# Softmax over a diagonal of dot products: whole-batch loads of x, half-batch loads of y, and one VectorE instruction for each row

## The chip, the cores and the metric

The kernel runs on one core of one Trainium2 chip. The metric is the device time of one execution in microseconds (us); each kernel is run several times, and the median is compared. The core has 16 DMA engines, which bring data from the chip's main memory (HBM) into the on-chip memory (SBUF, 128 partitions), and several compute engines of which this kernel uses VectorE (DVE), ScalarE (ACT) and GpSimd (POOL). SyncE (SP) computes nothing here; its queue issues the loads.

## The reference

```python
B, N, D = 8, 4096, 512            # x and y are [B, N, D], float32
gram = np.matmul(x, y.transpose(0, 2, 1))
diag = np.diagonal(gram, axis1=1, axis2=2)
diag = diag - diag.max(axis=-1, keepdims=True)
exp = np.exp(diag)
return exp / exp.sum(axis=-1, keepdims=True)
```

Only the diagonal of the product is used, so row n of a batch needs one dot product of 512 elements, x[b, n] . y[b, n]. A softmax over the 4096 dot products of each batch follows. The inputs are 2 x 64 MB (134.22 million bytes together), the output is 8 x 4096 numbers. Every input byte is used once.

## The kernel before

A batch of 4096 rows lies over 128 partitions, R = 32 consecutive rows on each. A partition's share of one tensor and one batch is thus 32 x 512 x 4 bytes = 64 KB, and it lies in one piece in HBM. The kernel handles a batch in two halves of H = 16 rows for each partition. For each half, `load` allocates a tile of x and one of y (32 KB in a partition each, 4 MB over all) and issues their loads on SP's queue, x at line 43 and y at line 44. The pool `io` has three buffers for each of the two, so SP can be up to three halves ahead. A load into a buffer waits until the instructions that read its former content are done.

The products and sums are made on VectorE in one of two ways. `dots` multiplies the whole half in one instruction, in place into the x tile (line 50), and adds up over the 512 elements in a second one (line 51). `dots_by_row` does each row of the half in one instruction that multiplies and accumulates (line 58), 16 instructions for a half. The last three halves go by row, all others by `dots`. The column of dot products goes to the tile `diag`, which keeps all batches.

After both halves of a batch, `softmax` takes the maximum over each partition (line 72, VectorE), over the partitions (line 74, GpSimd), negates it (line 76), takes the exponential with its sum (line 78, ScalarE), sums over the partitions (line 83, GpSimd), takes the reciprocal and scales (lines 85 and 86), and stores 16 KB from ScalarE's queue (line 87). These steps stand in VectorE's order between the products of one batch and those of the next.

The last two halves are loaded in pieces, so that little is left to do when the last bytes land: 8 and 8 rows for the first half of the last batch, and 8, 4, 2, 1 and 1 rows for its second half.

The order on each engine is the order of the program. The framework sets the semaphores; those for the ends of DMAs are eight, reused in turn, and a DMA that takes one up again waits until the DMA that had it before has landed. Both SP's loads and ScalarE's stores take from these eight.

Of the kernel before, what the change touches and what calls it, by code (L numbers as in the profile page):

```python
# [1 line left out]

# [5 lines left out]


@with_exitstack
def kernel(
    ctx: ExitStack,
    tc: tile.TileContext,
    x: bass.AP,
    y: bass.AP,
    out: bass.AP,
):
    nc = tc.nc
    f32 = mybir.dt.float32  # L20
    B, N, D = x.shape
    P = nc.NUM_PARTITIONS
    R = N // P
    H = R // 2


    xv = x.rearrange("b (p r) d -> b p r d", p=P)
    yv = y.rearrange("b (p r) d -> b p r d", p=P)
    ov = out.rearrange("b (p r) -> b p r", p=P)

    io = ctx.enter_context(tc.tile_pool(name="io", bufs=3))
    persist = ctx.enter_context(tc.tile_pool(name="persist", bufs=1))
    sm = ctx.enter_context(tc.tile_pool(name="sm", bufs=2))

    diag = persist.tile([P, B * R], f32, name="diag")
    res = persist.tile([P, B * R], f32, name="res")

    def load(b, r0, parts):
        xt = io.tile([P, H, D], f32, tag="xt", name="xt")
        yt = io.tile([P, H, D], f32, tag="yt", name="yt")  # L40
        o = 0
        for n in parts:
            nc.sync.dma_start(out=xt[:, o : o + n, :], in_=xv[b, :, r0 + o : r0 + o + n, :])  # L43
            nc.sync.dma_start(out=yt[:, o : o + n, :], in_=yv[b, :, r0 + o : r0 + o + n, :])  # L44
            o += n
        return xt, yt

    def dots(b, r0, xt, yt):
        c = b * R + r0
        nc.vector.tensor_tensor(out=xt, in0=xt, in1=yt, op=mybir.AluOpType.mult)  # L50
        nc.vector.tensor_reduce(  # L51
            out=diag[:, c : c + H], in_=xt, axis=mybir.AxisListType.X, op=mybir.AluOpType.add
        )

    def dots_by_row(b, r0, xt, yt):
        for k in range(H):
            c = b * R + r0 + k
            nc.vector.scalar_tensor_tensor(  # L58
                out=xt[:, k, :],
                in0=xt[:, k, :],  # L60
                scalar=1.0,
                in1=yt[:, k, :],
                op0=mybir.AluOpType.mult,
                op1=mybir.AluOpType.mult,
                accum_out=diag[:, c : c + 1],
            )

    def softmax(b):
        db = diag[:, b * R : (b + 1) * R]
        rb = res[:, b * R : (b + 1) * R]  # L70
        mxp = sm.tile([P, 1], f32, tag="mxp", name="mxp")
        nc.vector.tensor_reduce(out=mxp, in_=db, axis=mybir.AxisListType.X, op=mybir.AluOpType.max)  # L72
        mx = sm.tile([P, 1], f32, tag="mx", name="mx")
        nc.gpsimd.partition_all_reduce(out_ap=mx, in_ap=mxp, channels=P, reduce_op=bass_isa.ReduceOp.max)  # L74
        nmx = sm.tile([P, 1], f32, tag="nmx", name="nmx")
        nc.vector.tensor_single_scalar(out=nmx, in_=mx, scalar=-1.0, op=mybir.AluOpType.mult)  # L76
        sump = sm.tile([P, 1], f32, tag="sump", name="sump")
        nc.scalar.activation(  # L78
            out=rb, in_=db, func=mybir.ActivationFunctionType.Exp,
            bias=nmx, scale=1.0, accum_out=sump,  # L80
        )
        ssum = sm.tile([P, 1], f32, tag="ssum", name="ssum")
        nc.gpsimd.partition_all_reduce(out_ap=ssum, in_ap=sump, channels=P, reduce_op=bass_isa.ReduceOp.add)  # L83
        rc = sm.tile([P, 1], f32, tag="rc", name="rc")
        nc.vector.reciprocal(out=rc, in_=ssum)  # L85
        nc.vector.tensor_single_scalar(out=rb, in_=rb, scalar=rc, op=mybir.AluOpType.mult)  # L86
        nc.scalar.dma_start(out=ov[b], in_=rb)

    for b in range(B):
        for h in range(2):  # L90
            n = 2 * b + h
            parts = {2 * B - 2: [8, 8], 2 * B - 1: [8, 4, 2, 1, 1]}.get(n, [H])
            xt, yt = load(b, h * H, parts)
            (dots_by_row if n >= 2 * B - 3 else dots)(b, h * H, xt, yt)
        softmax(b)


# [1 line left out]
_INS = ['x', 'y']  # L99
_OUTS = [((8, 4096), 'float32')]  # L100


# [23 lines left out]
```

## Time and profile before

| | |
|---|---|
| device time, median of 3 runs | 323.48 us (323.29 to 323.94) |
| the profiled execution's own time | 323.94 us |
| its span, first to last instruction | 321.6 us |
| VectorE busy | 261.4 us, 81% of the span |
| ScalarE, GpSimd busy | 4.6 us, 6.1 us |
| moved by DMA | 134.36 MB, mean 418 GB/s over the span |
| loads issued by SP | 28 of 4 MB, 6 of 2 MB, 8 smaller |
| median time from issue to landing, 4 MB | 31.2 us (x), 40.5 us (y) |
| stores | 8 of 16 KB, median 12.9 us to landing |

The profile is of one execution. Its times are in microseconds from the start of the span; "busy" is the time in which an engine executes, and a line such as "L50" is the line of the program that made the instruction. A timeline row gives the start, the duration, the engine, the line, the operation with its output and inputs, and, in brackets, how long the engine stood idle before it and what ended that. "SPq" rows are the issue of a transfer, not the transfer itself. The difference between device time and span, 2.3 us here, lies outside the first and the last instruction.

### The profile page before, as it was taken

How to read it: one execution, taken by the hardware profiler on the slowest of the kernel's cores; microseconds unless marked ns; L12 is line 12 of the kernel's file. 1: busy time of each engine (PE TensorE's matmuls, PEld its weight loads, DVE VectorE, ACT ScalarE, POOL GpSimd, SP SyncE). 2: the span in 40 equal slices, each digit the busy share in tenths (PEclk: the TensorE clock that was granted, in tenths of full speed). 3: DMA queues.
4: the chain of work that ended last, by engine and by line, in shares of the span. 5: the costliest groups of instructions: out<-in, count | busy, mean ns of one | idle time of the engine just before them, and what ended most of it. 6: DMA issues, size and time to landing. Idle time of an engine off the chain costs nothing.

```text
span 321.6 us, 345 instructions
## 1 busy us (share of the span) xinstructions
DVE 261.4 (81%) x154; ACT 4.6 (1%) x17; POOL 6.1 (2%) x20
## 2 busy tenths in 40 slices
DVE  0019979898998979979799897989979799776494
ACT  1000000000000000000000000000000000000000
POOL 0000000000000000000000000000000000000000
DMA  8999999999999999999999999999999999999991
GB/s 326 456 395 452 440 408 456 391 458 391 456 412 436 454 395 456 440 408 458 416 432 456 392 458 440 408 456 417 433 449 395 456 437 412 424 424 426 427 407 53
DMA packets 7201, 134.36 MB, mean 418 GB/s; under 512 B 1824, under 2 KB 1824, under 8 KB 2592
## 3 DMA queue, kind: packets, MB, share of 16 engines
q1 hardware_dynamic: 6048, 134.22, 97.5%
q10 hardware_dynamic: 1152, 0.13, 0.3%
q14 instruction: 1, 0.01, 0.0%
HBM read 134.22 MB, written 0.13 MB: 418 GB/s over the span
## 4 chain that ended last, share of the span: by engine, by line
DMA 63%; DVE 33%; issue 1%; SPq 1%; POOL 1%; ACT 0%; POOLq 0%; DVEq 0%
DMA yt<-in_y_dram 63%; DVE xt L50 16%; DVE diag L51 16%; SPq L43 1%; POOL mx L74 0%; POOL ssum L83 0%; DVE mxp L72 0%; DVE xt L58 0%; ACT res L78 0%; DVE rc L85 0%; POOLq L121 0%; SPq L44 0%; DVE res L86 0%; DVE nmx L76 0%; DVEq L50 0%
## 5 line engine op out<-in xcount | busy, mean ns | idle before, releaser
L50 DVE TENSOR_TENSOR xt<-xt,yt 128x8192 f32<-128x8192 f32 x13 | 113.0, 8689 | 34.5 <-DMA yt<-in_y_dram 34.5
L51 DVE TENSOR_REDUCE diag<-xt 128x16 f32<-128x8192 f32 x13 | 112.9, 8686 | 0.4
L58 DVE SCALAR_TENSOR_TENSOR xt<-xt,yt 128x512 f32<-128x512 f32 x48 | 30.0, 687 | 9.9 <-DMA yt<-in_y_dram 9.7
L74 POOL PARTITION_ALL_REDUCE mx<-mxp x8 | 2.8, 352 | 306.6 <-DVE mxp L72 306.6
L85 DVE RECIPROCAL rc<-ssum 128x1 f32<-128x1 f32 x8 | 1.3, 164 | 7.7 <-POOL ssum L83 7.7
L78 ACT ACTIVATE res<-diag,nmx 128x32 f32<-128x32 f32 x8 | 2.6, 321 | 312.9 <-DVE nmx L76 312.9
L76 DVE TENSOR_SCALAR nmx<-mx 128x1 f32<-128x1 f32 x8 | 1.2, 154 | 4.3 <-POOL mx L74 4.3
L58 DVE DVE_READ_ACCUMULATOR xt<-xt,yt 128x1 f32 x48 | 3.9, 82 | 0.0
L83 POOL PARTITION_ALL_REDUCE ssum<-sump x8 | 3.1, 385 | 5.8 <-ACT res L78 5.8
L86 DVE TENSOR_SCALAR res<-res,rc 128x32 f32<-128x32 f32 x8 | 1.9, 242 | 0.9
L72 DVE TENSOR_REDUCE mxp<-diag 128x1 f32<-128x32 f32 x8 | 1.5, 186 | 0.3
L78 ACT ACTIVATION_READ_ACCUMULATOR res<-diag,nmx 128x1 f32 x8 | 1.5, 186 | 0.0
L78 ACT ACT_TABLE_LOAD x1 | 1.3, 1283 | 0.7 <-PEq L110 0.7
L110 POOL MEMSET const-float32-0.0<- 128x1 f32 x1 | 0.1, 100 | 0.2 <-issue 0.2
L110 POOL MEMSET const-bfloat16-1.0<- 128x1 bf16 x1 | 0.1, 102 | 0.0
L110 POOL MEMSET const-uint8-127<- 128x1 uint8 x1 | 0.1, 102 | 0.0
L110 POOL MEMSET const-float32-1.0<- 128x1 f32 x1 | 0.1, 99 | 0.0
## 6 DMA issues: line engine op xcount, KB each, us to landing
xt<-in_x_dram SPq DMA_DIRECT2D x14, 4096.0 KB, 31.2
yt<-in_y_dram SPq DMA_DIRECT2D x14, 4096.0 KB, 40.5
xt<-in_x_dram SPq DMA_DIRECT2D x3, 2048.0 KB, 27.1
yt<-in_y_dram SPq DMA_DIRECT2D x3, 2048.0 KB, 31.6
xt<-in_x_dram SPq DMA_DIRECT2D x1, 1024.0 KB, 31.9
yt<-in_y_dram SPq DMA_DIRECT2D x1, 1024.0 KB, 29.5
xt<-in_x_dram SPq DMA_DIRECT2D x1, 512.0 KB, 25.8
yt<-in_y_dram SPq DMA_DIRECT2D x1, 512.0 KB, 22.2
```

The costliest lines, as they stand in the source:

```text
L43: nc.sync.dma_start(out=xt[:, o : o + n, :], in_=xv[b, :, r0 + o : r0 + o + n, :])
L50: nc.vector.tensor_tensor(out=xt, in0=xt, in1=yt, op=mybir.AluOpType.mult)
L51: nc.vector.tensor_reduce(out=diag[:, c : c + H], in_=xt, axis=mybir.AxisListType.X, op=mybir.AluOpType.add)
L58: nc.vector.scalar_tensor_tensor(out=xt[:, k, :], in0=xt[:, k, :], scalar=1.0, in1=yt[:, k, :], op0=mybir.AluOpType.mult, op1=mybir.AluOpT ...
L72: nc.vector.tensor_reduce(out=mxp, in_=db, axis=mybir.AxisListType.X, op=mybir.AluOpType.max)
L74: nc.gpsimd.partition_all_reduce(out_ap=mx, in_ap=mxp, channels=P, reduce_op=bass_isa.ReduceOp.max)
L76: nc.vector.tensor_single_scalar(out=nmx, in_=mx, scalar=-1.0, op=mybir.AluOpType.mult)
L78: nc.scalar.activation(out=rb, in_=db, func=mybir.ActivationFunctionType.Exp, bias=nmx, scale=1.0, accum_out=sump,)
L83: nc.gpsimd.partition_all_reduce(out_ap=ssum, in_ap=sump, channels=P, reduce_op=bass_isa.ReduceOp.add)
L85: nc.vector.reciprocal(out=rc, in_=ssum)
L86: nc.vector.tensor_single_scalar(out=rb, in_=rb, scalar=rc, op=mybir.AluOpType.mult)
L110: nc = _bacc.Bacc("TRN2", target_bir_lowering=False, num_devices=1)
```

## The change

The tile of x now holds a whole batch (64 KB in a partition), is loaded by one DMA of 8 MB for the first seven batches, and has two buffers. The tile of y still holds a half (32 KB in a partition) and now has two buffers instead of three. On SP the loads of a batch are x, then the two halves of y. For the last batch x is loaded in pieces too, each ahead of its piece of y: 16 rows for the first half, then 8, 4, 2, 1 and 1 rows for the second. All halves are done by row (new line 47); the product is written in place into the y tile instead of the x tile. The two-instruction form is gone. The softmax is the same; its lines move up by 11.

```diff
--- before.py
+++ after.py
@@ -28,36 +28,25 @@
     yv = y.rearrange("b (p r) d -> b p r d", p=P)
     ov = out.rearrange("b (p r) -> b p r", p=P)
 
-    io = ctx.enter_context(tc.tile_pool(name="io", bufs=3))
+    io = ctx.enter_context(tc.tile_pool(name="io", bufs=2))
     persist = ctx.enter_context(tc.tile_pool(name="persist", bufs=1))
     sm = ctx.enter_context(tc.tile_pool(name="sm", bufs=2))
 
     diag = persist.tile([P, B * R], f32, name="diag")
     res = persist.tile([P, B * R], f32, name="res")
 
-    def load(b, r0, parts):
-        xt = io.tile([P, H, D], f32, tag="xt", name="xt")
-        yt = io.tile([P, H, D], f32, tag="yt", name="yt")
-        o = 0
-        for n in parts:
-            nc.sync.dma_start(out=xt[:, o : o + n, :], in_=xv[b, :, r0 + o : r0 + o + n, :])
-            nc.sync.dma_start(out=yt[:, o : o + n, :], in_=yv[b, :, r0 + o : r0 + o + n, :])
-            o += n
-        return xt, yt
+    def load_x(b, xt, r0, n):
+        nc.sync.dma_start(out=xt[:, r0 : r0 + n, :], in_=xv[b, :, r0 : r0 + n, :])
+
+    def load_y(b, yt, r0, o, n):
+        nc.sync.dma_start(out=yt[:, o : o + n, :], in_=yv[b, :, r0 + o : r0 + o + n, :])
 
     def dots(b, r0, xt, yt):
-        c = b * R + r0
-        nc.vector.tensor_tensor(out=xt, in0=xt, in1=yt, op=mybir.AluOpType.mult)
-        nc.vector.tensor_reduce(
-            out=diag[:, c : c + H], in_=xt, axis=mybir.AxisListType.X, op=mybir.AluOpType.add
-        )
-
-    def dots_by_row(b, r0, xt, yt):
         for k in range(H):
             c = b * R + r0 + k
             nc.vector.scalar_tensor_tensor(
-                out=xt[:, k, :],
-                in0=xt[:, k, :],
+                out=yt[:, k, :],
+                in0=xt[:, r0 + k, :],
                 scalar=1.0,
                 in1=yt[:, k, :],
                 op0=mybir.AluOpType.mult,
@@ -87,11 +76,19 @@
         nc.scalar.dma_start(out=ov[b], in_=rb)
 
     for b in range(B):
+        last = b == B - 1
+        xt = io.tile([P, R, D], f32, tag="xt", name="xt")
+        if not last:
+            load_x(b, xt, 0, R)
         for h in range(2):
-            n = 2 * b + h
-            parts = {2 * B - 2: [8, 8], 2 * B - 1: [8, 4, 2, 1, 1]}.get(n, [H])
-            xt, yt = load(b, h * H, parts)
-            (dots_by_row if n >= 2 * B - 3 else dots)(b, h * H, xt, yt)
+            yt = io.tile([P, H, D], f32, tag="yt", name="yt")
+            o = 0
+            for n in [8, 4, 2, 1, 1] if last and h == 1 else [H]:
+                if last:
+                    load_x(b, xt, h * H + o, n)
+                load_y(b, yt, h * H, o, n)
+                o += n
+            dots(b, h * H, xt, yt)
         softmax(b)
```

## The prediction

> **What bounds the kernel now.** I read the page first. Section 1 for the engines, section 2 for whether the transfers ever pause, section 3 for how they are cut.
>
> ```profile
> DVE 261.4 (81%) x154; ACT 4.6 (1%) x17; POOL 6.1 (2%) x20
> ...
> DMA  8999999999999999999999999999999999999991
> ...
> q1 hardware_dynamic: 6048, 134.22, 97.5%
> ```
>
> VectorE works 81% of the span, but the row of DMA tenths is at 9 from the second slice to the one before the last: the 16 DMA engines hardly rest. The load queue q1 moves 134.22 MB in 6048 packets. The program issues 42 loads, and 6048 / 42 = 144 = 128 + 16: one packet for each partition's run, and one small one for each DMA engine. So a packet is a run, 8 runs per DMA engine and load, and its length is what the kernel chose: 32 KB for 28 of the loads.
>
> Next the timeline of VectorE and of SP's queue in a steady stretch.
>
> ```profile
> 157.83 0.42 SPq L44 DMA_DIRECT2D yt<-in_y_dram  x1
> ...
> 159.17 8.69 DVE L50 TENSOR_TENSOR xt<-xt,yt 128x8192 f32<-128x8192 f32 x1 [1.75 <-DMA yt<-in_y_dram]
> ...
> 178.89 8.68 DVE L50 TENSOR_TENSOR xt<-xt,yt 128x8192 f32<-128x8192 f32 x1
> 187.61 8.69 DVE L51 TENSOR_REDUCE diag<-xt 128x16 f32<-128x8192 f32 x1
> ...
> 198.05 8.69 DVE L50 TENSOR_TENSOR xt<-xt,yt 128x8192 f32<-128x8192 f32 x1 [1.76 <-DMA yt<-in_y_dram]
> ...
> 236.93 8.69 DVE L50 TENSOR_TENSOR xt<-xt,yt 128x8192 f32<-128x8192 f32 x1 [1.75 <-DMA yt<-in_y_dram]
> ```
>
> Once a batch VectorE stands still and starts when y lands. These starts are 38.88 us apart, twice (198.05 - 159.17, 236.93 - 198.05): the beat of the transfers, 19.44 us for 8 MB of x and y (16 runs of 32 KB per DMA engine). The load issued at 157.83 is the one that lands for 198.05: it stood some 20 us behind another 8 MB. That is why the chain of waits shows 33% DVE and yet VectorE does not set the pace: an earlier issue would only stand longer in line.
>
> Last the end, where the runs become short.
>
> ```profile
> 276.67 0.69 DVE L58 SCALAR_TENSOR_TENSOR xt<-xt,yt 128x512 f32<-128x512 f32 x1 [2.07 <-DMA yt<-in_y_dram]
> ...
> 277.29 0.69 DVE L58 SCALAR_TENSOR_TENSOR xt<-xt,yt 128x512 f32<-128x512 f32 x1
> ...
> 296.27 0.69 DVE L58 SCALAR_TENSOR_TENSOR xt<-xt,yt 128x512 f32<-128x512 f32 x1 [2.43 <-DMA yt<-in_y_dram]
> ...
> 305.98 0.69 DVE L58 SCALAR_TENSOR_TENSOR xt<-xt,yt 128x512 f32<-128x512 f32 x1 [4.72 <-DMA yt<-in_y_dram]
> ...
> 316.15 0.69 DVE L58 SCALAR_TENSOR_TENSOR xt<-xt,yt 128x512 f32<-128x512 f32 x1 [0.50 <-DMA yt<-in_y_dram]
> ```
>
> From 276.67 to 296.27, 19.60 us, the same 8 MB arrive, now in runs of 16 KB (32 per DMA engine): 0.16 us more than 19.44, for 16 more packets and two more loads. So one packet more costs about 0.01 us; its bytes cost the rest. That is the price the whole forecast rests on. VectorE waits 4.72 us before 305.98 and 0.50 us before the last row at 316.15, so the last landing sets the end; the softmax and the store behind it take 321.6 - 316.15 = 5.45 us, and are untouched.
>
> **The change part by part.** The sum is made against the profiled execution: span 321.6, device time 323.94, 2.3 us outside the span. It is the slowest of the three runs shown (median 323.48, 0.46 less). 0.2% is 0.65 us, the spread of these runs, and about what a measurement can tell.
>
> *Runs of 64 KB for x.* Seven batches load x in 8 runs of 64 KB per DMA engine instead of 16 of 32 KB: 56 packets fewer, at 0.01 us, -0.56 us. No run here has a packet over 32 KB, so this is bounded. Best: -0.56, the step from 16 to 32 KB once more. Middle: the run goes out as two packets of 32 KB, 0. Worst: it is cut small. The nearest row is the last 8 rows of the batch, in runs of 8, 4 and 2 KB: 305.98 to 316.15 is 10.17 us where 8 rows at the steady beat take 9.72, so 4.6% more; on the x half of seven batches (7 x 19.44 = 136 us) that is +6.3 us. I take -0.56: the trace shows one packet for each run at every length used, and time per byte falling with length.
>
> *The last batch.* Its first half goes from two pieces of 8 rows to one of 16: 16 packets and two loads fewer, the measured 0.16 us the other way. *Fewer loads.* 7 more x loads disappear, 7 x 0.01 = -0.07 us (0 if nothing).
>
> [...]
>
> *VectorE.* The pair L50 and L51 costs 8.7 + 8.7 = 17.4 us per half. By row, starts are 277.29 - 276.67 = 0.62 us apart and 0.61 further on, 16 rows 9.8 us. In all 256 x 0.61 + 6 for the softmax = about 162 us instead of 261. All of it lies beside the transfers: a gain of 99 us on the engine, 0 on the path. [...]
>
> *Buffers and waits.* Can the queue now run empty? On SP the order becomes x0, y0a, y0b, x1, then y1a (waits until VectorE has left y0a), y1b (y0b), x2 (x0 free at the same moment), and so on. With 9.72 us per 4 MB: y0a lands near 32, its rows end near 42, and y1a is issued then, while x1 still streams until about 61: 19 us in hand. So in every batch, since x of the next batch always stands ahead. At the end x comes in pieces: y of the last batch's first half is issued when the y tile two back is done, near 275, with only its own x half before it, 9.7 us in hand; the 8 rows of y of the second half near 285, with some 14 us in hand. Each issue takes about 0.4 us. Cost 0; if VectorE were slower than 9.7 us per half plus that reserve, the shortfall would come straight on the path.
>
> *Semaphores of SP's loads.* They are reused every eight DMAs, the stores included. New is that a one-row piece of y near the end waits for the store of the seventh batch. It is issued near 288; the median store takes 12.9 us to land, so near 301, and the last y piece waits anyway for the 8-row piece, 10 us before the end, as it does now (305.98). Cost 0. A store that meets 64 KB packets may take up to twice as long, 26 us; only earlier batches' stores do, and nobody near them waits.
>
> *The end.* 16 rows by row (9.8 us) between landings 20 and 10.2 us before the end finish in time; 8, 4, 2 and 1 rows follow as now, and the 0.50 us wait before the last row is the cover. Cost 0, and up to 0.3 us if that cover is used up twice.
>
> *Sum:* -0.56 - 0.16 - 0.07 = -0.79 us. Span 321.6 to 320.8; profiled time 323.94 to 323.15; against the median 323.48 to **322.7 us**.
>
> **The rivals.**
>
> *Nothing to tell.* The change mainly frees VectorE, which is not the bound; if the long runs go out as two packets each, only the last batch gains: -0.16 - 0.07, 323.3 us. The saturated DMA row speaks for it, and the packet count per run against it. Also on this side: one step of the trace is 0.8 us late without a row that explains it (starts at 236.93 and 257.18, 20.25 us instead of 19.44); such a slip in some runs hides a gain of this size.
>
> *Slower: 64 KB packets stream at a lower rate than 32 KB ones.* Place: the x half of seven batches, 136 us. Each 1% costs 1.36 us, against 0.23 gained elsewhere: 323.48 - 0.23 + 1.36 = 324.6 us at 1%. Break-even is at 0.17%, and it is slower by over 0.2% from about 0.65%. No row excludes it, since no run is that long; the rows against it are those at 16 and 32 KB, where longer was quicker. Cut small, at 4.6%, it would be near 329.6.
>
> *VectorE as bound again or an empty queue.* At 0.61 us a row it would need three times the time per half to use up 19 us; I give it no chance of its own.
>
> **How the numbers follow.** Forecast (one packet per long run, -0.79): 0.58. Nothing to tell: 0.20. Slower: 0.22. The forecast lies only 0.14 us beyond the line of -0.65, so with the runs' scatter about 0.09 of its chance falls within 0.2%: 0.49 is left for faster. Of the rivals, 0.03 goes to faster for a slip that vanishes (0.01 from the second case, 0.02 from slower): faster 0.52, same 0.09 + 0.19 = 0.28, slower 0.20. The range starts at 321.9, where the 0.8 us slip also vanishes, and reaches to 324.4, which takes in the second case and slower packets up to about 0.85%. The likeliest case alone: 322.2 to 323.2.
>
> **What would show it.** Right: q1 with 33 loads and 7 x (128 + 16) + 26 x (128 + 16) = 4752 packets (5648 if long runs are split in two, far more if cut small); batch to batch starts of VectorE 38.79 us apart; the last batch's first 8 MB in 19.44 us; VectorE near 162 us busy; the last row near 315.4; the DMA row at 9 throughout. Wrong: a beat over 38.88 (slower packets), DMA tenths below 9 in the middle (an empty queue), or rows at the end that do not wait for a landing.

## The result, and the profile after

The changed kernel takes 325.14 us (median of 4 runs, 325.10 to 325.49) against 323.53 us before. The ratio is 1.0051, with a 95% interval of 1.0034 to 1.0068: half a percent slower, where 0.79 us less was forecast. The profiled execution took 325.13 us, its span is 323.1 us.

The page of the changed kernel, sections 1 to 3, the lines that answer to those shown of before, and one more:

```profile
DVE 163.9 (51%) x544; ACT 4.6 (1%) x17; POOL 6.1 (2%) x20
...
DMA  9899999899999999899999999899999899999980
...
q1 hardware_dynamic: 4752, 134.22, 96.6%
...
q14 instruction: 4, 0.03, 0.0%
```

VectorE is busy 163.9 us and the load queue moves 4752 packets, both as forecast; a 64 KB run is one packet (the packet records have 896 of 64 KB, 128 for each of the seven loads of 8 MB). The DMA row has six eights, the row of before one, in its first slice. The forecast had named such slices as the sign of an empty queue; they are none here, since the fastest kernel below has three of them too. New is the last line. Queue q14, whose kind the page calls instruction, moved 4 packets of 8 KB within the span; such a packet is called a block below. The same line of before, not shown in the forecast:

```profile
q14 instruction: 1, 0.01, 0.0%
```

The timeline of VectorE, changed kernel, at the instructions that wait for y of a batch's first half, and at the last row:

```profile
71.66 0.69 DVE L47 SCALAR_TENSOR_TENSOR yt<-xt,yt 128x512 f32<-128x512 f32 x1 [17.22 <-DMA yt<-in_y_dram]
...
110.38 0.69 DVE L47 SCALAR_TENSOR_TENSOR yt<-xt,yt 128x512 f32<-128x512 f32 x1 [16.72 <-DMA yt<-in_y_dram]
...
150.25 0.69 DVE L47 SCALAR_TENSOR_TENSOR yt<-xt,yt 128x512 f32<-128x512 f32 x1 [17.78 <-DMA yt<-in_y_dram]
...
188.98 0.69 DVE L47 SCALAR_TENSOR_TENSOR yt<-xt,yt 128x512 f32<-128x512 f32 x1 [16.64 <-DMA yt<-in_y_dram]
...
228.83 0.69 DVE L47 SCALAR_TENSOR_TENSOR yt<-xt,yt 128x512 f32<-128x512 f32 x1 [16.89 <-DMA yt<-in_y_dram]
...
267.59 0.69 DVE L47 SCALAR_TENSOR_TENSOR yt<-xt,yt 128x512 f32<-128x512 f32 x1 [16.67 <-DMA yt<-in_y_dram]
...
317.68 0.69 DVE L47 SCALAR_TENSOR_TENSOR yt<-xt,yt 128x512 f32<-128x512 f32 x1 [0.58 <-DMA yt<-in_y_dram]
```

The steps between batches are 38.72 (71.66 to 110.38), 39.87, 38.73, 39.85 and 38.76 us. Three of them are within 0.1 us of the 38.79 forecast; two are 1.1 us longer. The DMA view cut to the stretch 121 to 124 us, inside the first long step (columns: packets, MB, share):

```profile
q1 hardware_dynamic: 29, 1.90, 147.6%
q14 instruction: 1, 0.01, 0.7%
```

The trace's packet records put the four q14 packets at 48.3, 122.0, 195.8 and 271.9 us. Each of the two long steps holds one; the first packet falls into the step before the rows shown (32.42 to 71.66, 39.24 us), the fourth behind 267.59. In the kernel before the single one is at 241.1 us: inside the step from 236.93 to 257.18 that was 0.8 us late without a row to explain it.

The transfers' end, in the view by stretches (columns: stretch, its length, busy time and instructions of VectorE, ScalarE, GpSimd, granted clock, DMA share, GB/s):

```profile
306.00:311.00 5.00, 5.00 (x17) 0.00 (x0) 0.00 (x0) 1.00 1.00 407
311.00:313.50 2.50, 2.50 (x9) 0.00 (x0) 0.00 (x0) 1.00 1.02 377
314.30:317.10 2.80, 2.79 (x10) 0.00 (x0) 0.00 (x0) 1.00 0.06 25
```

In the last 2.8 us the DMA share is 0.06, which is 1/16: one DMA engine works alone, 15 are done. So the transfers did not get slower as a whole. One DMA engine fell behind, and since every load spreads over all 16 (144 packets, 9 x 16), each landing waited for that one.

The packet records allow this to be followed. Each load gives each DMA engine 8 packets of one size and one of 4 bytes, in a known order, so the packets can be chained engine by engine. The middle of the 16 engines ended its loads at 314.66 us before and at 313.58 us in the changed kernel, 1.1 us earlier. The last engine ended 1.0 us behind the middle before, and 3.6 us behind it after. Until the first q14 packet it was 0.2 us ahead of the middle; then its lag rises in steps, to 0.7, 1.7, 2.7 and 3.7 us, after the first, second, third and fourth q14 packet, and stays level between them.

The records also show what a step is made of. The q14 packet itself takes 0.31 to 0.33 us of its DMA engine. The load packet right behind it on that engine takes 1.88 us instead of 1.21 (32 KB), or 3.03 and 3.08 us instead of 2.42 (64 KB). Together that is 0.9 to 1.0 us. No other load packet of the changed kernel after the first 21 us is more than 0.25 us above the median of its size. Why the packet behind is slower is not shown.

### The profile page after: what moved, and what is told of

It is laid out like the page before. It is cut to its first block, busy times and chain, and to the rows that moved or that the text cites. A ratio compares the mean times of both kernels' runs of the same rounds, so it can differ in the third digit from the quotient of the medians.

```text
span 323.1 us, 714 instructions
## 1 busy us (share of the span) xinstructions
DVE 163.9 (51%) x544; ACT 4.6 (1%) x17; POOL 6.1 (2%) x20
## 3 DMA queue, kind: packets, MB, share of 16 engines
q1 hardware_dynamic: 4752, 134.22, 96.6%
## 4 chain that ended last, share of the span: by engine, by line
DMA 73%; DVE 25%; issue 1%; POOLq 0%; SPq 0%; POOL 0%; DVEq 0%
DMA yt<-in_y_dram 73%; DVE yt L47 25%; POOLq L118 0%; SPq L39 0%; POOL mx L63 0%; DVE res L75 0%; DVE mxp L61 0%; DVE rc L74 0%; DVEq L47 0%; DVEq L75 0%; POOLq L63 0%
## 5 line engine op out<-in xcount | busy, mean ns | idle before, releaser
L47 DVE SCALAR_TENSOR_TENSOR yt<-xt,yt 128x512 f32<-128x512 f32 x256 | 157.9, 687 | 143.8 <-DMA yt<-in_y_dram 143.8
L47 DVE DVE_READ_ACCUMULATOR yt<-xt,yt 128x1 f32 x256 | 21.0, 82 | 0.0
```

Of the source, the lines that this page charges most:

```text
L47: nc.vector.scalar_tensor_tensor(out=yt[:, k, :], in0=xt[:, r0 + k, :], scalar=1.0, in1=yt[:, k, :], op0=mybir.AluOpType.mult, op1=mybir.A ...
```

## The experiments

Theory 1: the 8 KB packets of q14 bring VectorE's instructions during the run, so that more rows mean more blocks; a block costs one DMA engine the 0.9 to 1.0 us read above, and as long as the queue stays full, this engine does not catch up. Theory 2: the long runs or the new order of loads make one engine lag. Theory 3: VectorE's traffic by row disturbs the transfers. The edits are shown shortened. Each kernel was timed beside the kernel before, whose median was 323.36 to 323.53 us every time.

**The long runs with the old VectorE mix.** Changed kernel, plus

```diff
+    def dots_pair(b, r0, xt, yt):      # tensor_tensor into yt, then tensor_reduce
-            dots(b, h * H, xt, yt)
+            (dots if 2 * b + h >= 13 else dots_pair)(b, h * H, xt, yt)
```

> The loads of the changed kernel, but the first 13 halves go by two instructions (product into the y tile, then the sum), the last 3 by row, as in the kernel before: 154 VectorE rows in the profile instead of 544. Theory 1 (instruction blocks: each 8 KB block that queue q14 brings delays one DMA engine by 0.8 to 1.0 us, and the lag stays to the end): q14 back to 1 packet, batch beat 38.80 us, median 323.53 - 0.8 = 322.7 us. Theory 2 (the 64 KB runs or the new load order let one DMA engine fall behind): 325.1 us, the last 3 us with one engine alone as in the changed kernel. Theory 3 (by-row VectorE traffic disturbs the transfers): 322.7 us too, so this run does not tell 1 from 3.

Measured: 323.99 us, from 322.58 to 325.13 over 12 runs; ratio 1.0012 (1.0000 to 1.0024). q14 fell to 1 packet, but only the fastest runs came to the 322.7 expected. This fits no theory as it stood. At the end one engine is late again:

```profile
315.00:316.00 1.00, 1.00 (x5) 0.00 (x0) 0.00 (x0) 1.00 0.06 25
```

SP's timeline has the issue of y for the 15th half:

```profile
282.65 0.33 SPq L42 DMA_DIRECT2D yt<-in_y_dram  x1
```

It is issued at 282.65 us, because the 13th half (two instructions, 17.4 us) holds its y buffer until then. The x half ahead of it runs out near 284, so the queue is all but empty. Whether that is the cause is tested further down, under "The old mix with the queue kept full".

**The old loads with every half by row.** Kernel before, with

```diff
-            (dots_by_row if n >= 2 * B - 3 else dots)(b, h * H, xt, yt)
+            dots_by_row(b, h * H, xt, yt)
```

> The kernel before with every half by row; loads and buffers untouched: 544 VectorE rows. Theory 1: q14 4 packets, 3 more than before at 0.8 to 1.0 us: 323.53 + 2.4 to 3.0 = 325.9 to 326.5 us, and the last 3 us of the transfers at a DMA share near 0.06. Theory 2: 323.5 us, nothing changes. Theory 3: slower, with the beat of every batch longer, not only of those with a q14 packet.

Measured: 326.38 us against 323.44, ratio 1.0093 (1.0080 to 1.0106). The loads are those of before to the byte, so theory 2 is out as the main cause. Its page and the last stretch of its transfers:

```profile
span 324.8 us, 730 instructions
...
DVE 164.5 (51%) x544; ACT 4.6 (1%) x17; POOL 6.1 (2%) x20
...
q14 instruction: 5, 0.04, 0.0%
```

```profile
315.00:317.90 2.90, 2.90 (x10) 0.00 (x0) 0.00 (x0) 1.00 0.07 25
```

Of the 5 packets, 4 come before the loads end and one at 322.4 us, behind them. Again one DMA engine is alone at the end. 2.94 us for 3 more blocks is 0.98 us each.

**The same number of instructions on another engine.** Kernel before, with

```diff
         nc.scalar.dma_start(out=ov[b], in_=rb)
+        if b < B - 1:
+            junk = sm.tile([P, 1], f32, tag="junk", name="junk")
+            for _ in range(55):
+                nc.scalar.activation(out=junk, in_=mx, func=Exp, bias=nmx, scale=1.0)
```

> The kernel before plus 55 one-column exponentials on ScalarE after each of the first seven softmaxes, whose result nobody reads; VectorE and loads untouched, ScalarE is idle there. Theory 1 with one DMA engine for all fetches: about 3 more q14 packets, 325.9 to 326.5 us. Theory 1 with another DMA engine for ScalarE's blocks: the two lags lie side by side, and 3 lags on one engine against 1 on the other give 323.53 + 1.6 to 2.0 = 325.1 to 325.5 us. Theories 2 and 3: 323.5 us.

Measured: 324.50 us against 323.44, ratio 1.0032 (1.0020 to 1.0044). VectorE and loads are untouched and ScalarE was busy for only 4.6 us before, so instructions alone cost time: theory 3 does not explain this. The size hit neither number. q14 has 4 packets (77.7, 184.1 and 262.6 us, within ScalarE's added instructions, and 241.9 us, where VectorE's came before). Chained by packet, two engines lag at the end of the loads: one 2.0 us (in three steps of 0.6 to 0.7) and another 1.0 us (one step). The end is set by the larger: 2.0 - 1.0 = 1.0 us more than before. So a block of ScalarE's costs less than one of VectorE's, and rides another DMA engine.

**Both at once.** The changed kernel with the same 55 instructions:

> The changed kernel plus the 55 unread one-column exponentials on ScalarE after each of the first seven softmaxes. VectorE's blocks (4) and ScalarE's (about 3) now come in one kernel. If ScalarE's blocks ride another DMA engine, whose smaller lag stays behind VectorE's: 325.1 us, no difference from the changed kernel, with q14 at 7 packets. If they ride the same one: 325.1 + 1.1 to 2.1 = 326.2 to 327.2 us (each ScalarE block at 0.35 us, what it cost on the kernel before, up to the 0.7 us that I read from its landings).

Measured: 325.47 us (325.03 to 326.00), ratio to before 1.0065 (1.0051 to 1.0079); the changed kernel's 1.0051 (1.0034 to 1.0068) overlaps it.

```profile
span 323.3 us, 1105 instructions
...
DVE 163.9 (51%) x544; ACT 117.0 (36%) x402; POOL 6.1 (2%) x20
...
q14 instruction: 7, 0.06, 0.0%
```

Seven packets, and no cost beyond the scatter. The lags of the two engines at the end of the loads are 3.7 and 1.9 us, side by side. ScalarE's blocks do ride another DMA engine.

**A dose between.** The changed kernel with the first 9, and then the first 5, halves by two instructions (the condition `>= 13` above made 9 and 5):

> The changed kernel with the first 9 halves by two instructions and 7 by row: 274 VectorE rows. Theory 1: blocks are brought at about 50, 174, 294 and 422 rows executed, so q14 2 packets, 322.7 + 0.9 = 323.6 us. Theory 2: 325.1 us. Theory 3: in proportion to the rows, 7 of 16 halves: some 322.7 + 2.4 x 4/13 = 323.4 us, but spread over the batches that go by row.

> The changed kernel with the first 5 halves by two instructions and 11 by row: 394 VectorE rows. Theory 1: blocks at about 50, 174 and 294 rows executed, q14 3 packets, 322.6 + 1.9 = 324.4 us, between the 323.26 of 274 rows and the 325.1 of 544.

Measured: 323.26 us (323.08 to 323.52) and 324.22 us (324.00 to 324.55), with 2 and 3 packets on q14, against 323.6 and 324.4 expected. The first time alone would fit theory 3 as well (323.4). The packet records do not: in both kernels one DMA engine's lag rises at the q14 packets (201.3 and 272.5 us; 153.0, 202.4 and 276.2 us) and is level between them, though VectorE goes by row there too. VectorE's busy times are 231.2 and 201.4 us, falling while the kernel gets slower.

**The old mix with the queue kept full.** As the first experiment, with

```diff
-            (dots if 2 * b + h >= 13 else dots_pair)(b, h * H, xt, yt)
+            (dots if 2 * b + h in (12, 14, 15) else dots_pair)(b, h * H, xt, yt)
```

> The changed kernel's loads with 154 VectorE rows again, but the halves by row are the 13th, 15th and 16th instead of the 14th to 16th, so that the y tile of the 13th half is free at about 275 us and its next load is issued with 9 us of x in hand, not 2. Theory 1: q14 1 packet, a clear gain, 322.6 us, within 0.3 us from run to run. If the 64 KB runs themselves let an engine fall behind (theory 2): 324.0 us and the scatter of the earlier run with 154 rows again.

Measured: 322.41 us (322.25 to 322.73) against 323.46, ratio 0.9968 (0.9956 to 0.9981). The 13th half now goes by row and frees its buffer early; SP's row for the same load is

```profile
275.73 0.33 SPq L42 DMA_DIRECT2D yt<-in_y_dram  x1
```

7 us earlier, and the scatter is gone. Loads and number of VectorE rows (154) are those of the first experiment, so moving that issue took its trouble away. The packet records of the first experiment show what the late issue did. By 284.98 us, 15 of the 16 DMA engines had begun this load. The last one stood idle from 284.13 us at the latest until 285.51 us, its first packet then took 2.64 us instead of 1.21, and the engine that ended last, 2.4 us behind the middle, traces back to that packet. Why just this engine got its work late is not settled. This kernel beats both others.

With these loads the four doses stand in a line:

| VectorE rows | q14 packets during the loads | median, us | step |
|---|---|---|---|
| 154 | 1 | 322.41 | |
| 274 | 2 | 323.26 | 0.85 |
| 394 | 3 | 324.22 | 0.96 |
| 544 (the changed kernel) | 4 | 325.14 | 0.92 |

The packet records agree. In the kernel before, in its version with every half by row, in the two kernels with ScalarE's extra instructions, and in the 154-row kernel of this table, the load packets after the first 21 us that take over 0.25 us more than the median of their size number 1, 4, 4, 7 and 1: as many as the blocks that came during the loads, each the next one of its engine behind a block. In the 274-row and 394-row kernels, in the first experiment and in the next one some more are slow, where a load of y was issued less than 3.5 us before its turn.

**The long runs by themselves.** The kernel above, with x of the first seven batches in two loads:

```diff
-            load_x(b, xt, 0, R)
+            load_x(b, xt, 0, H)
+            load_x(b, xt, H, H)
```

> The kernel of the clean run, but x of the first seven batches comes in two loads of 4 MB (32 KB runs) into the same 64 KB tile, one after the other. Buffers, order of bytes and VectorE's instructions are the same. If one packet costs 0.01 us: 56 packets and 7 loads more, 0.6 us, so 323.2 us and a beat of 38.88 instead of 38.80. If the length of the runs does nothing: 322.6 us.

Measured: 323.10 us (322.69 to 323.59); ratio to before 0.9988 (0.9980 to 0.9997). The long runs are worth 323.10 - 322.41 = 0.69 us; 0.63 was expected. The two intervals leave anything from about 0.2 to 1.2 us, and seven of the slow packets named above, behind late loads of y, are in this run and none in the kernel above. The packet records give a second reading: at the middle DMA engine a steady batch takes 38.80 us in the changed kernel and 38.86 us in the kernel before, 0.06 us less, or 0.4 us over seven batches.

**Fewer VectorE instructions in the kernel before.** `n >= 2 * B - 3` made `n >= 2 * B - 2`:

> The kernel before with only the last two halves by row: 122 VectorE rows instead of 154. Theory 1, if a block is brought once about 50 rows have been executed: still q14 1 packet, 323.4 us, no difference. If a block is only brought when the program has more than 128 rows: q14 none, 322.6 us.

Measured: 323.21 us against 323.46, ratio 0.9991 (0.9982 to 1.0000); q14 still has its packet, at 240.6 us, so trimming 30 rows (to 124 in the profile) saves no block. In all these runs VectorE's first block within the span comes with 45 to 74 of its instructions begun. Whether a program with fewer VectorE instructions than lie between two blocks of the changed kernel, 126 to 132, would need none stays open: with those that do not count as busy, 35 in the trace of the kernel before, this one still has 159.

## Why the prediction was wrong, point by point

- **The failed step: VectorE.** "All of it lies beside the transfers: a gain of 99 us on the engine, 0 on the path." The engine's time was right (163.9 us) and is indeed beside the transfers. Its instructions are not: 390 more rows are 3 more blocks, and these come through the DMA engines that set the end. The term was +2.73 us instead of 0: the changed kernel's 325.14 less the 322.41 of the kernel with the same loads and 154 rows. With the -1.05 measured for the loads the sum is -1.05 + 2.73 = +1.68; the changed kernel measured +1.61.
- **What the profile had shown.** The line "q14 instruction: 1" stood on the page, and the one late step stood in the timeline. I called it a slip "without a row that explains it", and asked whether it would vanish; the DMA view cut to that step names it.
- **The 64 KB runs and fewer loads**, -0.63 forecast: -0.69 by the medians, -0.4 by the steady batch. Right in direction and within the noise in size. The slower rival (long packets at a lower rate) is out: the undisturbed steps are 38.72 to 38.76 us.
- **All the loads together**, -0.79 forecast: 322.41 against 323.46, -1.05 (interval -1.4 to -0.6). Right within that interval.
- **Buffers, semaphores, the end**: right for the changed kernel. The middle DMA engine ended 1.1 us earlier than before, and VectorE waited 0.58 us for the last row (0.50 before). A store took 14.3 us to land in the median and 15.2 at most, not up to 26. The reserve I counted at the end, 9.7 us, was about 6.3: y was issued at 277.50 us, and its x half ran out near 283.8. It is also what the by-row form buys: with the two-instruction form in the 13th half it shrinks to under 2 us, and the runs spread over 2.5 us (322.58 to 325.13).
- **The direction.** It came out slower, the case given 0.20, but not by the mechanism I named for it.
- **The blocks, for VectorE and for the transfers.** In the changed kernel the four blocks come 126, 126 and 132 VectorE instructions apart, with those that do not count as busy. No wait of VectorE names one: its waits are for y (143.8 us) and for GpSimd's two steps (12.0 us). The cost is in the transfers: with DMA engines that are busy all the time (a share of 1.00 from 60 to 110 us) each of VectorE's blocks cost 0.85 to 0.98 us.

## What to carry to other kernels

When the DMA engines are busy from end to end, look at the last stretch: here the slowest of them set the end, and a DMA share of 0.06, near 1/16, in the last 2.8 us said that one engine was alone. Count the instructions of every engine, also of one that is off the path: 390 more on VectorE brought 3 more blocks and cost 2.73 us, 385 more on ScalarE brought 3 and cost 1.06 us (324.50 against 323.44), through the DMA engines that carry the loads. A lag did not shrink while the queue was full: in the changed kernel it was 0.7, 1.7, 2.7 and 3.7 us after the four blocks, and level between them. So an engine freed of work can make a transfer-bound kernel slower, if the work is cut into many more instructions: VectorE's busy time fell from 261.4 to 163.9 us, and the time rose from 323.53 to 325.14 us.

## What the runs showed of the hardware that was not expected

- An instruction block is one packet of 8 KB (0.3 us by the packet records), yet sets its DMA engine back by 0.9 to 1.0 us for VectorE and 0.6 to 0.7 us for ScalarE. The rest is in the load packet right behind it, which takes 0.60 to 0.66 us longer than its like behind a block of VectorE's and 0.34 to 0.38 us longer behind one of ScalarE's.
- All of VectorE's blocks hit the same DMA engine of a run, and ScalarE's another: with 4 and 3 of them in one kernel the lags were 3.7 us on one engine and 1.9 us on another, and the time, 325.47 us, was within the scatter of that with the 4 alone, 325.14.
- Packets of 64 KB stream at the rate of shorter ones (2.42 us against 1.21 for 32 KB): 56 packets and 7 loads fewer saved 0.4 to 0.7 us, about 0.01 us for each.
